# Weight blocks requested one token tile sooner, with a mark before their conversions, and separate staging tiles for the modulation slices

## Chip, cores and metric

The kernel runs on one core of one Trainium2 chip. The metric is the device time of one execution in microseconds (us); the median of several runs is compared.

## The reference

The kernel computes a decoder trunk of two layers on 1024 tokens of width 1024, in float32. Cut to what matters, one layer is

```python
shift, scale, gate = split(c_act @ w_mod + b_mod, 3)
h = rms_norm(x, pre_gain) * (1 + scale) + shift
proj = h @ w_in                      # 1024 x 1024 times 1024 x 3088
# columns of proj: attention (aq, ak, av, ag), retention (rq, rk, rv, rg),
# gated linear attention (gq, gk, gv, gg, ga)
a_out = sliding_window_attention(rot(aq), rot(ak), av, sinks) * silu(ag)
r_out = rms_norm(retention(rot(rq), rot(rk), rv)) * silu(rg)
g_out = rms_norm(gated_linear_attention(gq, gk, gv, log_a(ga)), gain) * silu(gg)
y = concat(a_out, r_out, g_out) @ w_out
x = x + gate * rms_norm(y, post_gain)
```

Attention has 8 heads of 64 with a window of 128 tokens, retention 4 heads of 64 in chunks of 128, gated linear attention 4 heads in chunks. `c_act` is one vector, so that the modulation is a product of one vector with a matrix of 1024 x 3072 for each layer.

## The kernel before

**Units.** The 1024 tokens are eight tiles of 128. The columns of `w_in` and `w_out` are cut into units of 256 columns (`UNITS`): gg, rg, rq, rk, rv, gqk, gv, kv, aq0, aq1, ag0, ag1 and o0 to o3. A unit's weights are held in SBUF as two float32r halves, a high part and a low part (the rest of the rounding), and a product takes three passes: high times high, low times high, high times low (`PASSES`). A tile of a unit is so 3 x 8 matmuls of 128x256 (`project`, line 619), or of 128x512 where the unit is the stationary side (`project_T`).

**Places.** The units lie in a few slots of two large tiles (`arena0`, `arena1`), and each slot serves several units in turn (`PLACE`): gg, rk, gv, aq1 and ag1 one slot, rg, rv, kv, ag0 another, rq, gqk, aq0 a third. A unit can be written only after the last matmul that reads the unit before it in its slot. The order of work in a layer is: gg and rg over all tiles, then for each of four pairs of tiles rq, rk and rv, then gqk, gv and kv, then aq0 and aq1, ag0 and ag1, and the output.

**Loading a unit.** `load` (line 508) makes four requests, one for each chunk of 256 KB. A request has two halves. The first, `issue`, takes a staging tile `st` of 128x512 and issues the chunk's DMA from SyncE's queue. The second, `conv`, writes the high part to the slot (chunk 0 on VectorE, chunks 1 to 3 on ScalarE, lines 149 and 151) and then the low part (chunks 0 to 2 on VectorE, chunk 3 on GpSimd, line 533). With the last chunk it sets the flag `("w", l, name)`, for which `used` (line 504) waits before the unit's first matmul. The requests go through one queue, and the job `loader` (line 474) takes one step each 1.2 us of the planner's clock: an issue, or, when three chunks are in flight (`LAG`, 2, plus 1), first the conversion of the oldest. The call of `load` stands behind the last tile of the unit that held the slot before: in `do_gates` for rk and rv, in the retention loop for gqk, gv and kv, in `do_gqk`, `do_gv` and behind `do_kv` for aq0, aq1 and ag0. These are eight units in each of the two layers. The other units (gg, rg, rq, ag1, o0 to o3, and the last layer's `sw_first`) are requested elsewhere.

**Staging tiles.** There are five `st` tiles (`BST`). They hold the weight chunks, and also the slices of `w_mod`: `mod_third` (line 343) goes through a third of a layer's modulation in two halves of eight slices of 256 KB each; each slice is multiplied by one column of `c_act` and added to `acc` on VectorE (lines 362 and 364). 64 slices come so, at steps of 4.0 us of the planner (`mod2`), from the end of the first layer's gates to the end of the second layer's retention. The post-norm gain (line 377) takes an `st` tile too. Late in the second layer `last_output` uses `st` tiles as scratch and for one operand (`a22`, line 1311).

**What sets the order.** TensorE's instructions run in the order in which the program writes them out. A planner in the kernel makes that order: it has a clock that each matmul advances by an estimate, jobs that wait for a time or a flag, and `pump` (line 210), called every seven matmuls, which runs the jobs that are due. The other engines' instructions and the DMAs are put in order by the framework, in a list made when the program is compiled: it follows the order of the program where several are ready, and waits for tiles to come free. [...] Almost all DMAs are issued by SyncE.

**The retention core**, which the prediction speaks of: `ret_core` (line 1160) transposes a tile of queries and keys on TensorE, copies them out of PSUM on ScalarE (line 1169), multiplies them (the eight matmuls of 64x128), masks the scores on VectorE (line 1179) and adds the state `stR` (lines 1198 and 1200).

## Time and profile before

| what | us |
|---|---|
| median of three runs | 998.21 (996.72 to 999.19) |
| the profiled execution, its own time | 996.31 |
| its span from first to last instruction | 994.6 |
| TensorE busy | 965.7 |
| VectorE busy | 683.2 |
| ScalarE busy | 409.3 |
| GpSimd busy | 246.3 |

The profile is that of the one execution of 996.31 us; 1.7 us of it lie outside the span. PE is TensorE, DVE VectorE, ACT ScalarE, POOL GpSimd, and SPq SyncE's queue of DMA issues. A row of a timeline gives the start, the duration, the engine, the line, the operation, what it writes and reads, the shape, the number of like instructions merged into the row, and in brackets how long the engine was idle before and what ended the wait. A row of a list of waits gives who waited for what, the sum in us, the number of times and the longest. A group of the page's fifth part gives the number of instructions, their busy time in us, the mean of one in ns and the idle time before them. L165 is the helper through which every matmul goes, L180 that of transposes, L149 and L151 those of copies on ScalarE and VectorE, L154 that of DMAs.

### The profile page before, as it was taken

How to read it: one execution, taken by the hardware profiler on the slowest of the kernel's cores; microseconds unless marked ns; L12 is line 12 of the kernel's file. 1: busy time of each engine (PE TensorE's matmuls, PEld its weight loads, DVE VectorE, ACT ScalarE, POOL GpSimd, SP SyncE). 2: the span in 40 equal slices, each digit the busy share in tenths (PEclk: the TensorE clock that was granted, in tenths of full speed). 3: DMA queues.
4: the chain of work that ended last, by engine and by line, in shares of the span. 5: the costliest groups of instructions: out<-in, count | busy, mean ns of one | idle time of the engine just before them, and what ended most of it. 6: DMA issues, size and time to landing. Idle time of an engine off the chain costs nothing.

```text
span 994.6 us, 19641 instructions
## 1 busy us (share of the span) xinstructions
PE 965.7 (97%) x7133; PEld 824.3 (83%) x7133; DVE 683.2 (69%) x1679; ACT 409.3 (41%) x1152; POOL 246.3 (25%) x310
## 2 busy tenths in 40 slices
PE   5899999999999999999999999999999999999996
PEld 1599999888998777778889999988999877777785
DVE  3779857677766777664677286775766577567876
ACT  2477312233332656632555332133333257574222
POOL 2322001233310234420124101113322034545000
PEclk8899999999999999999999999999999999999999
DMA  9843513523135355587555241352122434378883
GB/s 321 290 138 97 159 44 115 177 86 121 61 100 166 91 157 168 170 274 239 189 170 171 69 150 38 118 157 83 53 93 86 127 91 133 112 235 266 267 262 139
DMA packets 112305, 148.77 MB, mean 150 GB/s; under 512 B 12065, under 2 KB 63821, under 8 KB 112209
## 3 DMA queue, kind: packets, MB, share of 16 engines
q1 hardware_dynamic: 106512, 137.96, 44.5%
q10 hardware_dynamic: 5696, 9.56, 2.6%
q8 instruction: 56, 0.92, 0.4%
q14 instruction: 41, 0.33, 0.1%
HBM read 109.20 MB, written 36.18 MB: 146 GB/s over the span
## 4 chain that ended last, share of the span: by engine, by line
PE 80%; DVE 7%; DMA 7%; issue 2%; POOL 1%; ACT 1%; SPq 0%; ACTq 0%; POOLq 0%; DVEq 0%
PE mm L165 61%; PE aux L165 14%; PE aux L180 5%; DMA st<-in_w_in_dram 2%; POOL sm L635 1%; DMA t<-aoS 1%; DMA st<-in_w_last_dram 1%; DMA xk<-in_x_dram 1%; DVE arena L533 1%; DMA a<-mixS 1%; DVE t L1248 0%; DVE t L328 0%; DMA t<-in_x_dram 0%; DMA t<-xs 0%; DMA mixS<-t 0%
## 5 line engine op out<-in xcount | busy, mean ns | idle before, releaser
L165 PE MATMUL mm<-arena 128*128 128x256 f32 (+2 forms) x1824 | 299.9, 318 | 1.8 <-ACT arena L704 1.8
L165 PE MATMUL mm<-arena,arena 128*128 128x256 f32 (+2 forms) x1824 | 298.2, 316 | 0.0
L165 PEld LDWEIGHTS mm<-arena 128*128 128x128 f32 x1824 | 255.5, 191 | 26.0 <-issue 3.3
L165 PEld LDWEIGHTS mm<-arena,arena 128*128 128x128 f32 x1824 | 252.2, 188 | 24.3 <-issue 3.7
L635 POOL TENSOR_TENSOR sm<-sm,mhalf 128x1 f32<-128x1 f32 (+1 forms) x64 | 55.8, 872 | 335.9 <-DVE sm L634 317.8
L165 PE MATMUL mm<-arena,mx 128*128 128x512 f32 (+1 forms) x564 | 130.6, 387 | 0.5 <-ACT kept L1341 0.5
L165 PEld LDWEIGHTS mm<-arena,mx 128*128 128x128 f32 x564 | 101.4, 188 | 24.7 <-issue 1.9
L149 ACT ACTIVATE t<-aux 128x256 f32<-128x256 f32 (+2 forms) x124 | 55.8, 468 | 73.8 <-PE aux L180 62.2
L149 ACT ACTIVATE arena<-st 128x512 fp32r<-128x512 f32 x94 | 56.2, 627 | 53.2 <-DMA st<-in_w_in_dram 19.4
L929 POOL TENSOR_TENSOR smx<-smx,sm 128x512 f32<-128x512 f32 x32 | 36.1, 1129 | 125.7 <-DVE sm L928 118.0
L533 POOL TENSOR_TENSOR arena<-st,arena 128x512 fp32r<-128x512 f32 x31 | 42.7, 1378 | 79.7 <-ACT arena L149 72.9
L533 DVE TENSOR_TENSOR arena<-st,arena 128x512 fp32r<-128x512 f32 x77 | 58.0, 775 | 5.2 <-ACT arena L149 3.3
L925 ACT ACTIVATE smx<-smx,sm 128x129 f32<-128x129 f32 x128 | 49.9, 393 | 25.9 <-DVE sm L922 25.7
L364 DVE SCALAR_TENSOR_TENSOR acc<-st,c_act,acc 128x512 f32<-128x512 f32 x60 | 46.7, 778 | 16.9 <-DMA st<-in_w_mod_dram 16.5
L180 PE MATMUL aux<-c_ident,t 128*128 128x128 f32 (+1 forms) x292 | 48.2, 282 | 5.4 <-DVE t L666 5.0
L180 PEld LDWEIGHTS aux<-c_ident,t 128*128 128x128 f32 (+1 forms) x292 | 35.0, 144 | 12.4 <-DVE t L666 6.9
L698 ACT ACTIVATE t<-aux,mod,mod 128x128 f32<-128x128 f32 x68 | 25.9, 459 | 43.0 <-DVE t L1248 18.1
L165 PEld LDWEIGHTS aux<-t,mx 32*128 32x128 f32 (+1 forms) x896 | 39.5, 187 | 3.9 <-issue 2.1
L973 ACT ACTIVATE t<-aux 128x256 f32<-128x256 f32 x32 | 12.3, 383 | 73.6 <-PE aux L165 65.0
L165 PE MATMUL aux<-t,mx 32*128 32x32 f32 (+1 forms) x896 | 40.7, 272 | 0.0
L920 DVE COPY_PREDICATED smx<-c_curmask,aux 128x256 f32<-128x256 int32 x64 | 25.4, 446 | 19.5 <-ACT smx L149 17.2
L1248 DVE SCALAR_TENSOR_TENSOR t<-t,sm,t 128x512 f32<-128x512 f32 x32 | 24.0, 780 | 18.2 <-DMA t<-in_x_dram 10.8
(224 smaller groups left out, 1387.7 us busy)
## 6 DMA issues: line engine op xcount, KB each, us to landing
st<-in_w_in_dram SPq DMA_DIRECT2D x96, 256.0 KB, 3.8
st<-in_w_mod_dram SPq DMA_DIRECT2D x64, 256.0 KB, 3.1
mx<-mixS SPq DMA_DIRECT2D x20, 512.0 KB, 4.9
mixS<-t SPq DMA_DIRECT2D x72, 128.0 KB, 3.7
st<-in_w_last_dram SPq DMA_DIRECT2D x36, 256.0 KB, 3.8
wm<-in_w_mod_dram SPq DMA_DIRECT2D x12, 512.0 KB, 7.0
t<-in_x_dram SPq DMA_DIRECT2D x24, 256.0 KB, 4.9
t<-tabS SPq DMA_DIRECT2D x16, 256.0 KB, 4.6
```

The lines of the kernel that those rows point to most:

```text
L149: A.activation(dst, src, AF.Copy)
L165: T.matmul(dst, lhsT, rhs, start=start, stop=stop)
L180: T.transpose(dst, src, idn)
L364: V.scalar_tensor_tensor(acc, wt, c_act[:, k:k + 1], acc, ALU.mult, ALU.add)
L533: e.tensor_tensor(lo, st, f(hi), ALU.subtract)
L635: G.tensor_tensor(r, r, mhalf[:, :w], ALU.pow)
L698: A.activation(hf[:, ks], at[kt], AF.Identity, scale=gain, bias=shift)
L920: V.copy_predicated(sv, curmask.unsqueeze(1).to_broadcast((P, 2, P)), pv[:, :, n // P - 1, :])
L925: A.activation(sm[:, h, :], sm[:, h, :], AF.Exp, bias=mx[:, h:h + 1], accum_out=sums[:, h:h + 1])
L929: eng("pn").tensor_tensor(sm[:, :, 0:128], sm[:, :, 0:128], rs.unsqueeze(2).to_broadcast((P, 4, P)), ALU.mult)
L973: A.activation(sq, po, AF.Square)
L1248: V.scalar_tensor_tensor(xt[j], yg[j], r, xt[j], ALU.mult, ALU.add)
```

## The change

1. The eight calls of `load` stand ahead of the last tile's matmuls (for aq0 ahead of the last `project_T`) of the unit that holds the slot, and are followed by a `pump`.
2. Such a request carries a mark, `gate`, the flag `("end", l, name)`. It is set where the call of `load` stood before. The loader issues as long as no more than three chunks are in flight; when it would convert a chunk whose mark isn't set, it waits for the mark.
3. `mod_third` takes its slices and gains from three tiles of their own (`mod_stage`, tag `sm8`, `BMOD`, 3). The five `st` tiles stay.
4. The program is built with `dynamic_dma_scratch_size=1024`.

The planner's delays (`L`), the table of engines (`EN`) and `LAG` stay as they are. The diff, cut where the same edit is repeated:

```diff
+    def mod_stage():
+        return gp.tile([P, 512], F32, tag="sm8", name=nm("ms"), bufs=BMOD)
...
             for k in range(KT):
-                wt = stage()
+                wt = mod_stage()
                 dma("lwm", wt, w_mod[l, j, hh, :, k, :])
...
-                gain = stage()
+                gain = mod_stage()
...
     def convert():
-        conv, st = flying.pop(0)
+        conv, st, gate = flying.pop(0)
+        assert gate is None or gate in flags
         conv(*st)
+
+    def gated():
+        g = flying[0][2]
+        return g is not None and g not in flags
 
     def loader(l):
         while queue or flying:
             if queue:
-                n, issue, conv = queue.pop(0)
-                while flying and sum(len(s) for _, s in flying) + n > LAG + 1:
+                n, issue, conv, gate = queue.pop(0)
+                while flying and sum(len(s) for _, s, _ in flying) + n > LAG + 1:
+                    if gated():
+                        yield (0.0, flying[0][2])
                     convert()
-                flying.append((conv, issue()))
+                flying.append((conv, issue(), gate))
                 yield lat("ld1", l)
             else:
+                if gated():
+                    yield (0.0, flying[0][2])
                 convert()
                 yield lat("ld2", l)
...
         def do_gates(name, p):
             w = used(l, name)
             for t in (2 * p, 2 * p + 1):
+                if t == NT - 1:
+                    load(l, "rk" if name == "gg" else "rv", gate=("end", l, name))
+                    pump()
                 pg = mm()
...
             if p == NP_ - 1:
-                load(l, "rk" if name == "gg" else "rv")
+                flag(("end", l, name))
...
                 for tt in range(2):
                     t = 2 * p + tt
+                    if t == NT - 1:
+                        load(l, {"rq": "gqk", "rk": "gv", "rv": "kv"}[name], gate=("end", l, name))
+                        pump()
                     pm = mm()
...
-                if last:
-                    load(l, {"rq": "gqk", "rk": "gv", "rv": "kv"}[name])
+                if t == NT - 1:
+                    flag(("end", l, name))
...
-B2, B1, BS, BST, MMB, SMB = 10, 8, 11, 5, 3, 3
+B2, B1, BS, BST, MMB, SMB, BMOD = 10, 8, 11, 5, 3, 3, 3
...
-    nc = _bacc.Bacc("TRN2", target_bir_lowering=False, num_devices=1)
+    nc = _bacc.Bacc("TRN2", target_bir_lowering=False, num_devices=1, dynamic_dma_scratch_size=1024)
```

`do_gqk`, `do_gv` and `do_kv` are changed like `do_gates`, with aq0, aq1 and ag0.

More of the change, by code (lines that the diff above doesn't have):

```diff
@@ L490, in drain, with request @@
         while queue:
-            n, issue, conv = queue.pop(0)
-            while flying and sum(len(s) for _, s in flying) + n > LAG + 1:
+            n, issue, conv, gate = queue.pop(0)
+            while flying and sum(len(s) for _, s, _ in flying) + n > LAG + 1:
                 convert()
-            flying.append((conv, issue()))
+            flying.append((conv, issue(), gate))
         while flying:
             convert()
-    def request(l, n, issue, conv):
-        queue.append((n, issue, conv))
+    def request(l, n, issue, conv, gate=None):
+        queue.append((n, issue, conv, gate))
         if not loading[0]:
@@ L506, in used, with load @@
         return unit(l, name)
-    def load(l, name, first=None):
+    def load(l, name, first=None, gate=None):
         if l >= DEPTH:
@@ L547, in load @@
             else:
-                request(l, 1, lambda kc=kc: issue(kc), lambda st, kc=kc: conv(kc, st))
+                request(l, 1, lambda kc=kc: issue(kc), lambda st, kc=kc: conv(kc, st), gate)
     def sw(name):
@@ L1502, in layer @@
         for p in range(NP_):
-            last = p == NP_ - 1
             rr = {}
@@ L1526, in do_gqk @@
         def do_gqk(hf, kk):
+            if hf and kk:
+                load(l, "aq0", gate=("end", l, "gqk"))
+                pump()
             pm = mm()
@@ L1538, in do_gqk @@
             if hf and kk:
-                load(l, "aq0")
+                flag(("end", l, "gqk"))
         def do_gv(p):
             for t in (2 * p, 2 * p + 1):
+                if t == NT - 1:
+                    load(l, "aq1", gate=("end", l, "gv"))
+                    pump()
                 pm = mm()
@@ L1550, in do_gv @@
             if p == NP_ - 1:
-                load(l, "aq1")
+                flag(("end", l, "gv"))
         def do_kv(p):
@@ L1556, in do_kv @@
             for t in (2 * p, 2 * p + 1):
+                if t == NT - 1:
+                    load(l, "ag0", gate=("end", l, "kv"))
+                    pump()
                 pk = mm()
@@ L1572, in layer @@
             do_kv(p)
-        load(l, "ag0")
+        flag(("end", l, "kv"))
         job(attn_run(l))
```

## The prediction

> **What bounds the kernel now.** I read the page's first part, then TensorE's waits after the start-up, then the timelines of the engines around the longest of them.
>
> ```profile
> span 994.6 us, 19641 instructions
> PE 965.7 (97%) x7133; PEld 824.3 (83%) x7133; DVE 683.2 (69%) x1679; ACT 409.3 (41%) x1152; POOL 246.3 (25%) x310
> 50.00:994.60 944.60, 930.03 (x6994) 805.15 (x6992) 654.60 (x1615) 390.66 (x1107) 231.02 (x287) 1.00 0.46 141
> ```
> ```profile
> PE aux L165 <- ACT t L149: 3.0, 3, 1.3
> PE mm L165 <- DMA a<-mixS: 1.5, 1, 1.5
> PE mm L165 <- ACT kept L1341: 0.5, 1, 0.5
> PE aux L165 <- DVE sm L634: 0.4, 1, 0.4
> PE aux L165 <- DVE t L1179: 0.4, 1, 0.4
> PE aux L165 <- DVE stR L1200: 0.3, 1, 0.3
> PE aux L180 <- DVE mx L1121: 0.2, 1, 0.2
> ```
>
> TensorE is the bound. Past 50 us it is busy for 930.03 of 944.60 us at a granted clock of 1.00, and the second fence, which is every wait of TensorE over 0.15 us in that stretch, adds up to 3.0 + 1.5 + 0.5 + 0.4 + 0.4 + 0.3 + 0.2 = 6.3 us. The change removes no matmul, so it can give back only a part of these 6.3 us. The page's chain of waits also names DMA of in_w_in_dram with 2% of the span (some 20 us), but most of that time lies beside a running TensorE, so I take the waits and not the chain as the measure.
>
> Which of them have to do with weights? These are TensorE's rows with an idle time, first layer and second layer, and ScalarE (ACT) just ahead of them.
>
> ```profile
> 192.83 0.71 PE L165 MATMUL aux<-t 64*128 64x128 f32 x8 [1.29 <-ACT t L149]
> ...
> 663.09 0.71 PE L165 MATMUL aux<-t 64*128 64x128 f32 x8 [0.54 <-ACT t L149]
> ...
> 669.66 0.71 PE L165 MATMUL aux<-t 64*128 64x128 f32 x8 [1.22 <-ACT t L149]
> ...
> 673.62 0.46 PE L165 MATMUL aux<-stR,t 128*128 128x128 f32 x2 [0.30 <-DVE stR L1200]
> ...
> 674.62 0.43 PE L165 MATMUL aux<-t,t 128*128 128x64 f32 x2 [0.37 <-DVE t L1179]
> ```
> ```profile
> 189.35 0.63 ACT L149 ACTIVATE arena<-st 128x512 fp32r<-128x512 f32 x1 [1.72 <-DMA st<-in_w_in_dram]
> ...
> 191.39 0.63 ACT L149 ACTIVATE arena<-st 128x512 fp32r<-128x512 f32 x1 [1.14 <-DMA st<-in_w_in_dram]
> ```
> ```profile
> 661.10 0.63 ACT L149 ACTIVATE arena<-st 128x512 fp32r<-128x512 f32 x1 [0.90 <-DMA st<-in_w_in_dram]
> 661.64 0.64 ACT L149 ACTIVATE t<-aux 128x256 f32<-128x256 f32 x2
> ...
> 668.49 0.63 ACT L149 ACTIVATE arena<-st 128x512 fp32r<-128x512 f32 x1 [3.71 <-DMA st<-in_w_in_dram]
> 669.03 0.58 ACT L149 ACTIVATE t<-aux 128x512 f32<-128x512 f32 x1
> ```
>
> The reader is to see a queue. The eight 64x128 matmuls are the retention scores (ret_core), and they need the copy of line 1169. That copy stands on ScalarE behind the conversion of a weight chunk, and the conversion stands still until the chunk's DMA has landed: 3.71 us at 668.49, 1.72 and 1.14 us at 189.35 and 191.39. No matmul needs those weights yet; they only sit ahead of something that a matmul does need. The two VectorE waits at 673.62 and 674.62 follow in the same place, where VectorE too was held by late chunks. So the part of the 6.3 us that this change aims at is 1.29 + 0.54 + 1.22 + 0.30 + 0.37 = **3.72 us**, all of it in the last retention pair of the two layers.
>
> **Why those chunks are late.** SyncE's timeline shows when they are asked for.
>
> ```profile
> 155.72 0.33 SPq L154 DMA_DIRECT2D st<-in_w_in_dram  x1
> ...
> 161.96 0.33 SPq L154 DMA_DIRECT2D st<-in_w_mod_dram  x1
> 162.75 4.50 SPq L154 DMA_DIRECT2D st<-in_w_in_dram  x3
> ...
> 171.64 0.33 SPq L154 DMA_DIRECT2D st<-in_w_mod_dram  x1
> ...
> 174.34 0.33 SPq L154 DMA_DIRECT2D st<-in_w_mod_dram  x1
> ...
> 181.84 4.82 SPq L154 DMA_DIRECT2D st<-in_w_in_dram  x3
> ...
> 187.24 0.38 SPq L154 DMA_DIRECT2D st<-in_w_in_dram  x1
> ```
> ```profile
> SPq L154 <- DVE arena L533: 7.3, 6, 3.4
> SPq L154 <- DVE acc L364: 6.9, 5, 3.9
> ```
> ```profile
> 170.20 1.68 ACT L149 ACTIVATE arena<-st 128x512 fp32r<-128x512 f32 x3 [3.70 <-PE mm L165]
> ```
>
> gqk's chunks are issued from 155.72 on, though the call that asks for them stands behind rq's last tile, whose matmuls end at 170.2 (the conversions wait for them there). The issue is thus already some 14 us ahead of its place in the code: what holds it is a free staging tile, not the request. Between 160 and 200 us SyncE stands 7.3 us until a conversion's low half (L533) and 6.9 us until a modulation product (L364) gives a tile back. kv's four chunks go out at 181.84 to 187.24 and are wanted at 187 to 190.
>
> **The change part by part.**
>
> *Three staging tiles for the modulation slices.* Nothing is computed that wasn't; 64 slices and 4 gains move to their own tiles, the five old ones hold weights alone. At 181.84 the queue was let go by a modulation product, so the last chunks go out earlier by about the time of the tiles lent out: three slices sit between gqk's and kv's chunks, up to the 6.9 us above. The waits of 1.1 to 3.7 us on landing are shorter than that, so I count them as gone, with TensorE's 3.72 us behind them. Three tiles instead of a share of five could starve the slices.
>
> ```profile
> L364 DVE SCALAR_TENSOR_TENSOR acc<-st,c_act,acc 128x512 f32<-128x512 f32 x60 | 46.7, 778 | 16.9 <-DMA st<-in_w_mod_dram 16.5
> ...
> st<-in_w_in_dram SPq DMA_DIRECT2D x96, 256.0 KB, 3.8
> st<-in_w_mod_dram SPq DMA_DIRECT2D x64, 256.0 KB, 3.1
> ```
>
> A slice lands 3.1 us after its issue and its product takes 0.78 us, so three tiles carry a slice every (3.1 + 0.8) / 3 = 1.3 us; the planner spaces them by 4.0 us (mod2). VectorE already waits 16.5 us for slices, and TensorE's seven waits name none of these products. Cost: nothing, hidden by VectorE's own idle third; between -0.4 us (the one wait on L634 goes too) and +1.3 us (a slice on the path of one retention tile).
>
> *Requests one tile sooner.* Sixteen requests (rk, rv, gqk, gv, kv, aq0, aq1, ag0 in two layers) stand ahead of the last project instead of behind it. At most three chunks are issued before the mark (LAG), the fourth after it. By 155.72 against 170.2 above the issues are not held by the request, so by itself this is worth nothing. SyncE's queue keeps its number of DMAs; the four issues of a request, 0.33 us each, can only move ahead of stores of mixS and loads of srS, and no wait of TensorE in the list above names those. The pump that comes with a request runs at the clock of the pump before it, so only the loader moves in it, and the loader emits no matmul and no clock: TensorE's order stays as it is.
>
> *The mark.* Before, a unit's four conversions came 3.6 to 7.2 us behind the request in the planner's clock (steps of 1.2, ld1 and ld2); now the first comes at the first pump after the mark, the last about 3 us sooner than before. In the lists of ScalarE, VectorE and GpSimd they so come ahead of work that stood ahead of them. Each still waits for the last tile's matmuls. Behind the waiting conversion stand ScalarE's copies out of PSUM, and for these TensorE waits. A unit's conversions are three on ScalarE at 0.63 us, one cast and three low halves on VectorE and one low half on GpSimd:
>
> ```profile
> L533 DVE TENSOR_TENSOR arena<-st,arena 128x512 fp32r<-128x512 f32 x77 | 58.0, 775 | 5.2 <-ACT arena L149 3.3
> ```
>
> On VectorE three times 0.78 us come sooner, ahead of rotations that the scores want later; there the planner leaves room, since a key's rotation is done two tiles before its scores. No row shows a mark. Its price is between nothing and one wait like that at 669.66 (1.22 us) for each of 16 units, 19.5 us. I take three ends that cost what 663.09 cost, 3 x 0.54 = 1.6 us, since the conversions at 170.20 stood 3.70 us behind TensorE and cost TensorE nothing: nearer the low end.
>
> *Descriptor scratch cut to 1024.*
>
> ```profile
> q1 hardware_dynamic: 106512, 137.96, 44.5%
> q10 hardware_dynamic: 5696, 9.56, 2.6%
> ```
>
> The program's DMAs run on these two hardware queues, issued by SyncE and ScalarE, and its table of issuing engines (EN) gives none to GpSimd, so I count nothing. [...]
>
> **Sum.** -3.72 + 1.6 = -2.1 us: span 992.5, the execution's own time 996.31 - 2.1 = 994.2. That execution was 1.9 us under the median of the three runs (998.21, they lie from 996.72 to 999.19); from the median, **996.1 us**. A difference under 0.3%, 3.0 us, I take as no change that can be told.
>
> **Rivals.**
>
> *All of it comes (0.30).* The mark costs nothing, as at 170.20: 998.21 - 3.7 = 994.5, or 993.0 if one more of the other waits goes (a<-mixS, 1.5). For it: these conversions run at the same release before and after.
>
> *The low halves hold the ring, not the slices (0.17).* The 7.3 us behind L533 are the larger of the two rows, and 187.24 was let go by such a half. Then kv's last chunk still lands near 191 and the 1.29 and 0.54 stay; 1.9 goes, 1.6 comes: 997.9. That the sooner request does not bring the data sooner belongs here.
>
> *ScalarE stands behind TensorE in place of the DMA (0.15, slower).* A marked conversion at the head of ScalarE's queue, as at 170.20, with a copy for the scores or an attention tile behind it: 1.2 us an end. From the third end on it eats the gain, from six on it is a loss over 0.3%: 6 x 1.25 - 3.7 = +3.8, 1002.0. Against it: TensorE's waits show no such case in 16 ends.
>
> *VectorE and GpSimd in each other's way (0.05).*
>
> ```profile
> 178.23 0.42 DVE L979 TENSOR_TENSOR t<-t,t 128x256 f32<-128x256 f32 x1
> ...
> 183.39 0.85 DVE L979 TENSOR_TENSOR t<-t,t 128x256 f32<-128x256 f32 x1
> ```
> ```profile
> 182.65 1.30 POOL L533 TENSOR_TENSOR arena<-st,arena 128x512 fp32r<-128x512 f32 x1
> ```
>
> The same instruction takes 0.42 us alone and 0.85 us beside GpSimd's low half. If the sooner conversions bring every unit's GpSimd half beside an instruction that TensorE waits for, that is 16 x 0.43 = 6.9, less 3.7: 1001.4. The number of such halves does not change and most of them delay nothing that TensorE wants, hence the small chance. [...]
>
> **Numbers.** My forecast has 0.33, the rivals 0.30, 0.17, 0.15 and 0.05 with it make one. Under 995.2 lies most of the first rival and a little of the forecast: faster 0.33. Over 1001.2 lies most of the third and half of the fourth: slower 0.17. Within 0.3%: 0.50. The range goes from the low end of the first rival, 993.0, to 1001.0, which leaves out most of the two slow cases and little else.
>
> **What would show it.** Right: kv's last chunk is issued before 184 us in the first layer and before 661 in the second; ScalarE's waits for in_w_in_dram in those pairs are gone; TensorE's waits at 193, 663 and 670 as well, and its list after 50 us is near 4 us. Wrong: new rows of TensorE waiting on ACT L149 with ScalarE waiting on PE mm ahead of them (third rival), chunks let go by L533 as late as now (second), or VectorE's products waiting longer than 16.5 us with TensorE behind them. Outside all this would be a span that falls by more than the 6.3 us of waits.

## The result and the profile after

The changed kernel takes 1009.45 us (median of six runs, 1006.92 to 1014.10), the kernel before beside it 997.81 (996.56 to 999.19): a ratio of 1.0121, with a 95% interval of 1.0102 to 1.0141, so **12 us slower**. The forecast was 996.1, and its range ended at 1001.0.

The first two lines are the page of the changed kernel, the third is its row of the windows view for the time past 50 us (busy time of PE, PEld, DVE, ACT, POOL, then the granted clock, the transfers' share and GB/s); the second fence is its list of TensorE's waits in that time.

```profile
span 1005.2 us, 19645 instructions
PE 969.1 (96%) x7133; PEld 826.9 (82%) x7133; DVE 681.5 (68%) x1679; ACT 409.7 (41%) x1152; POOL 246.4 (25%) x310
50.00:1005.20 955.20, 934.82 (x6999) 808.94 (x6997) 653.59 (x1617) 391.60 (x1109) 231.60 (x288) 0.99 0.46 140
```
```profile
PE aux L183 <- DVE t L678: 5.3, 2, 4.0
PE aux L168 <- ACT t L152: 2.1, 2, 1.2
PE mm L168 <- DMA a<-mixS: 1.6, 2, 1.4
PE aux L168 <- DVE t L1191: 1.5, 1, 1.5
PE aux L168 <- DVE mx L1133: 0.4, 1, 0.4
```

The five engines do the same number of instructions (the counts in the second line are those of before); past 50 us the stretch is 955.20 - 944.60 = 10.6 us longer. TensorE idles 955.20 - 934.82 = 20.4 us there in place of 14.6, so **5.8 us are new waits**; and it is busy for 4.8 us longer with the same matmuls, at a mean clock of 0.99 in place of 1.00, so **4.8 us are slower matmuls**. That second half has no place in the prediction at all. It isn't peculiar to the profiled run: the mean granted clock is 0.985 over the changed kernel's six runs and 0.990 over the 91 runs of the kernel before that were taken beside the experiments. Counting what is missing to 1.00 as time at half clock, that is 30 us against 19, so about 6 of the 12 us (my estimate).

**The waits.** The row of 5.3 us is new: two waits (1.22 and 4.04 us) at the hand-over of the layers, where the second layer's rows are normalised (L678; L666 before) as the first layer's output comes out. The row for L152 and the one for L1191 are the second layer's last retention pair. TensorE and ScalarE there, in the changed kernel:

```profile
672.96 0.71 PE L168 MATMUL aux<-t 64*128 64x128 f32 x8 [0.89 <-ACT t L152]
678.20 0.77 PE L168 MATMUL aux<-t,t 128*128 128x64 f32 x4 [1.46 <-DVE t L1191]
681.38 0.71 PE L168 MATMUL aux<-t 64*128 64x128 f32 x8 [1.24 <-ACT t L152]
```
```profile
670.97 0.63 ACT L152 ACTIVATE arena<-st 128x512 fp32r<-128x512 f32 x1 [3.34 <-DMA st<-in_w_in_dram]
676.46 0.63 ACT L152 ACTIVATE arena<-st 128x512 fp32r<-128x512 f32 x1 [3.56 <-DMA st<-in_w_in_dram]
```

The picture is that of before, and larger: 0.89 + 1.46 + 1.24 = 3.59 us where 2.43 stood, and ScalarE still stands on chunks that haven't landed. Only the first layer's 1.29 us at 193 is gone.

**The hand-over.** SyncE's rows, of the kernel before and then of the changed one:

```profile
447.65 0.33 SPq L154 DMA_DIRECT2D aoS<-t  x1
450.22 0.93 SPq L154 DMA_DIRECT2D t<-aoS  x2
...
451.79 0.86 SPq L154 DMA_DIRECT2D t<-in_x_dram  x2
...
486.69 0.98 SPq L154 DMA_DIRECT2D t<-in_x_dram  x2
```
```profile
443.62 1.09 SPq L157 DMA_DIRECT2D ms<-in_w_mod_dram  x2
...
449.59 0.33 SPq L157 DMA_DIRECT2D aoS<-t  x1
454.65 0.93 SPq L157 DMA_DIRECT2D t<-aoS  x2
...
456.22 0.86 SPq L157 DMA_DIRECT2D t<-in_x_dram  x2
...
489.84 1.12 SPq L157 DMA_DIRECT2D ms<-in_w_mod_dram  x2
491.05 1.67 SPq L157 DMA_DIRECT2D t<-in_x_dram  x2
...
493.72 1.27 SPq L157 DMA_DIRECT2D ms<-in_w_mod_dram  x2
```

SyncE's longest wait from 484 to 492 us in the changed kernel, and the two waits behind it:

```profile
SPq L157 <- DVE sm L652: 5.3, 1, 5.3
```
```profile
498.96 0.75 DVE L1260 SCALAR_TENSOR_TENSOR t<-t,sm,t 128x512 f32<-128x512 f32 x1 [3.36 <-DMA t<-in_x_dram]
```
```profile
508.96 1.97 PE L183 MATMUL aux<-c_ident,t 128*128 128x128 f32 x8 [4.04 <-DVE t L678]
```

In the kernel before no slice is loaded between 435.8 and 534.4 us: the last part's slices share the five tiles with weight chunks and stand behind them. With tiles of their own they are free to go, and the list that the framework writes for SyncE puts them among the loads of the residual `x`. The store of an attention tile goes out 1.9 us later, its reload and the load of `x` behind it 4.4 us later (456.22 against 451.79), while TensorE is 1.1 us late there (its transposes at 456.1 against 455.0). Then SyncE stands 5.3 us, up to 489.84, before the next two slices. The list names a small VectorE instruction; the slice's product that gives a tile back ends at the same moment (VectorE's row at 489.07 lasts 0.74 us), so I read it as a wait for one of the slices' own three tiles. The load of `x` stands behind, and goes out at 491.05 where it was 486.69. Two more slices follow it at 493.72, so four slices of 256 KB are issued within 5 us, around it. Its second half, issued at 492.39, lands 6.6 us later (498.96) and VectorE stands 3.36 us for it; in the kernel before VectorE had both halves at 490.96, 4.3 us after the first was issued, without a wait for them. The fifth token tile is late by that, and TensorE waits 4.04 us. VectorE also has five products of slices to do from 489.07 to 507.3, about 3.7 us that it did not have there before; no run separates them from the loads.

**The clock.** Three stretches of the windows view behind that wait:

```profile
504.60:508.00 3.40, 0.32 (x2) 0.00 (x0) 3.37 (x9) 3.14 (x10) 0.48 (x1) 1.00 0.75 253
508.00:511.40 3.40, 2.44 (x10) 2.34 (x11) 2.98 (x8) 1.63 (x6) 0.39 (x1) 0.51 0.53 192
511.40:514.80 3.40, 3.40 (x9) 2.62 (x9) 2.95 (x6) 0.91 (x2) 0.99 (x1) 0.50 0.45 162
```

From 508.0 on, for 6.8 us, the granted clock is 0.50, and in the last of the three stretches nine matmuls fill what sixteen filled before. In the kernel before no such stretch lies between 46 and 991 us (granted clock 1.00).

### The profile page after: what moved, and what is told of

Same layout as the page of the kernel before. It is cut to its first block, busy times and chain, and to the rows that moved or that the text cites. A ratio compares the mean times of both kernels' runs of the same rounds, so it can differ in the third digit from the quotient of the medians.

```text
span 1005.2 us, 19645 instructions
## 1 busy us (share of the span) xinstructions
PE 969.1 (96%) x7133; PEld 826.9 (82%) x7133; DVE 681.5 (68%) x1679; ACT 409.7 (41%) x1152; POOL 246.4 (25%) x310
## 4 chain that ended last, share of the span: by engine, by line
PE 62%; DMA 8%; DVE 8%; ACT 2%; issue 2%; POOL 1%; SPq 0%; ACTq 0%; POOLq 0%; DVEq 0%
PE mm L168 46%; PE aux L168 13%; PE aux L183 3%; DMA t<-in_x_dram 2%; DMA st<-in_w_in_dram 1%; DMA st<-in_w_last_dram 1%; DMA t<-aoS 1%; POOL sm L647 1%; DVE t L1260 1%; DMA ms<-in_w_mod_dram 1%; DMA aoS<-t 1%; DMA a<-mixS 1%; DMA t<-mixF 1%; ACT t L710 1%; DVE acc L367 1%
## 5 line engine op out<-in xcount | busy, mean ns | idle before, releaser
L152 ACT ACTIVATE t<-aux 128x256 f32<-128x256 f32 (+2 forms) x124 | 55.9, 468 | 77.1 <-PE aux L183 61.2
L152 ACT ACTIVATE arena<-st 128x512 fp32r<-128x512 f32 x94 | 56.1, 628 | 56.4 <-PE mm L168 22.6
L545 DVE TENSOR_TENSOR arena<-st,arena 128x512 fp32r<-128x512 f32 x77 | 58.7, 786 | 6.1 <-ACT arena L152 4.3
L545 POOL TENSOR_TENSOR arena<-st,arena 128x512 fp32r<-128x512 f32 x31 | 43.5, 1403 | 78.6 <-ACT arena L152 69.8
L367 DVE SCALAR_TENSOR_TENSOR acc<-ms,c_act,acc 128x512 f32<-128x512 f32 x60 | 46.0, 767 | 15.9 <-DMA ms<-in_w_mod_dram 15.4
```

The costliest lines, as they stand in the source:

```text
L152: A.activation(dst, src, AF.Copy)
L367: V.scalar_tensor_tensor(acc, wt, c_act[:, k:k + 1], acc, ALU.mult, ALU.add)
L545: e.tensor_tensor(lo, st, f(hi), ALU.subtract)
```

## The experiments

Three theories. **A**: the slices' own tiles cost, since they take a brake off the slices, whose loads and products now run ahead into the hand-over and into the first core of the gated attention. **B**: the mark costs, since the conversions stand earlier in ScalarE's, VectorE's and GpSimd's lists than their chunks land. **C**, in the first two expectations: half from each. In those of e8_delay, e10_fill_after and e11_fill_start C is the name of another theory, formed after the first four profiles: a wait costs more than itself because the clock is halved after it. All runs of the kernel before with other tiles also have the smaller scratch; e13_scratch_only tells what that alone does. Ratios are to runs of the kernel before on the same chip (997.8, 997.4, 996.6, 996.7, 997.1 and 997.2 us in the six groups of runs), with their 95% interval.

### One part alone, and parts of the first part

**e1_tiles_only.** The kernel before with the own tiles (and the smaller scratch), no mark.

```diff
-                wt = stage()
+                wt = mod_stage()
...
-                gain = stage()
+                gain = mod_stage()
```

> The kernel before with the modulation slices in three tiles of their own and the smaller descriptor scratch, requests and marks as before. Theory A (the own tiles let the last layer's modulation slices run ahead into the change from the first layer to the second, where they stand before the loads of x on SyncE's queue and before the residual on VectorE): slower by most of the 11.6 us, 1006 to 1011, with a wait of TensorE of 3 us or more on DVE t (the normalised rows) near 505 us, a stretch at half the granted clock behind it, and slices issued before 500 us. Theory B (the marked conversions or the shifted requests delay ScalarE and VectorE): within 0.3% of before, 995 to 1001. Theory C (both parts cost a half each): 1002 to 1005.

1009.96 us, 1.0142 (1.0109 to 1.0175): **the whole loss**, with TensorE's order unchanged. TensorE waits 2.43 us at the hand-over, 0.89 us at 222 us, and 0.95 + 1.42 + 1.32 us in the second layer's last retention pair. The half clock that theory A expected behind the hand-over isn't there: the 56 matmuls of 128x512 behind that wait take 13.29 us from 510.84 on, 13.27 in the kernel before. In this profile it stands at 224.8 us (0.50 up to 228.2), and behind the last pair's last wait, from 680.97 on, twelve matmuls of 128x512 take 5.14 us where the kernel before has 3.02.

**e2_mark_only.** The changed kernel with slices and gains back in the shared tiles.

```diff
-                wt = mod_stage()
+                wt = stage()
...
-                gain = mod_stage()
+                gain = stage()
```

> The changed kernel with the modulation slices back in the five shared tiles; requests one tile sooner and marks stay. Theory A: no loss of the kind, 994 to 1000, and no half clock between 50 and 900 us. Theory B: 1006 to 1011. Theory C: 1002 to 1005. Either way the chunks of kv should not be issued earlier than before by more than 2 us, since a free tile holds them and not the request.

1008.05 us, 1.0112 (1.0087 to 1.0137). No wait at the hand-over; but 3.62 us at 197, and in the second layer's last pair 0.38, 1.35 and 2.16:

```profile
676.02 0.63 ACT L152 ACTIVATE arena<-st 128x512 fp32r<-128x512 f32 x1 [3.83 <-DMA st<-in_w_in_dram]
...
679.79 0.63 ACT L152 ACTIVATE arena<-st 128x512 fp32r<-128x512 f32 x1 [1.85 <-DMA st<-in_w_in_dram]
```
```profile
683.73 0.43 PE L168 MATMUL aux<-t,t 128*128 128x64 f32 x2 [2.16 <-DVE t L1191]
```

Each part alone costs about what both cost together (by the medians 10 and 12 against 12 us), so the two do not add up; half from each is out. Theory A had 994 to 1000 us here, so it is not the whole account.

**e3_last_gate_shared.** The changed kernel with the last layer's third part (the gate's 16 slices and 2 gains) back in the shared tiles. **e4_held.** The changed kernel with that part's loads placed behind the first layer's last load of `x`.

```diff
-                wt = mod_stage()
+                wt = mod_stage() if (l, j) != (1, 2) else stage()
```
```diff
+                if (l, j) == (1, 2):
+                    with tc.issue_after(lastx[0].ins):
+                        dma("lwm", wt, w_mod[l, j, hh, :, k, :])
```

> The changed kernel, but the sixteen gate slices of the second layer take the five shared tiles again, where they must stand in turn behind the weight chunks asked for before them. The other 48 slices keep their own tiles. Theory A: the wait of TensorE near 505 us and the half clock behind it vanish, 996 to 1002. Theory B: unchanged, 1006 to 1011.

> The changed kernel with all own tiles, but each DMA of the second layer's gate slices is placed on SyncE's queue behind the first layer's last load of x. Theory A: as in the kernel with the shared tiles for these slices or better, 995 to 1001, with the slices issued after 515 us and no half clock near 505. If the slices' products alone and not their place before the loads of x were the cause this gives the same, since the products follow the slices. Theory B: 1006 to 1011.

1003.66 us, 1.0065 (1.0042 to 1.0087), and 1005.22, 1.0084 (1.0063 to 1.0105). In both the hand-over is clean; in the profile of e4_held the transposes come at 503.98 without a wait:

```profile
503.98 1.03 PE L183 MATMUL aux<-c_ident,t 128*128 128x128 f32 x8
```

Theory A had up to 1002 and up to 1001 us, so it foretold more than came; theory B had 1006 to 1011, too much, if by little for e4_held. 4 to 6 of the 12 us hang on where that part's loads stand. The hold moves the slices' products along with their loads, so it doesn't tell the two apart; that VectorE stands 3.36 us for `x` speaks for the loads.

**e9_first_own.** As e1_tiles_only, with the last layer's third part on the shared tiles (the edit of e3_last_gate_shared, no mark). **e14_tiles_held.** As e1_tiles_only, with the hold of e4_held. **e13_scratch_only.** The kernel before with the smaller scratch alone.

> The kernel before with the three own tiles and no mark, but the last layer's third modulation part (the gate and its gains) left on the shared tiles. Theory A with its place at the hand-over: against the 1010 of the own tiles alone, the waits at 472 and 510 go (0.33 and 2.43 us) and what is left is the wait of 0.89 at 222 with its half clock, so 999 to 1004 us. If the whole loss of the own tiles came from the last layer's third part: 995 to 998 us. If it came from the first layer's slices: 1006 to 1010 us.

> The three own tiles, no mark, and the loads of the last layer's third modulation part placed behind the last load of the first layer's residual tiles on SyncE's list. Theory A, as refined by the profiles (SyncE stood 5.3 us at 484 to 490 us on a slice's load that waited for its own tile, with the residual's loads queued behind it): against the 1010 of the own tiles alone, the waits at 473 and 510 go and it is 1001 to 1005 us, near the 1000.5 of the run in which those slices stayed on the shared tiles. If the slices' products on VectorE, not their loads on SyncE, made the rows late: still 1007 to 1010.

> The kernel before with only the smaller GpSimd scratch of the change (1024), which stands in every run with own or more tiles and in those with the mark; no instruction differs. The prediction's step (the scratch costs nothing): 996 to 998.5 us. If the scratch itself costs, the readings of those runs fall by as much.

1000.46 us, 1.0037 (1.0016 to 1.0058); 1005.44, 1.0084 (1.0054 to 1.0114); 997.90, 1.0010 (0.9993 to 1.0028). The scratch costs nothing that can be told. Without the mark the last third part on own tiles costs 9 us by the medians (10 by the ratios, 1.0142 - 1.0037); moving its loads out of the hand-over gives back 3 to 6 (1.0142 - 1.0084 is the larger; one of the four runs of e1_tiles_only, 1016.14 us, draws its ratio up). In the profile the hold brings a new wait of 1.25 us at 540, and the last pair's 0.96 + 1.35 + 1.13 us are about what they were; why the rest of the loss stays is not shown. With the loads held, the mark adds nothing (e4_held and e14_tiles_held have the same ratio).

### The mark

**e6_mark_late.** As e2_mark_only, with the conversions let go 3.6 us of the planner's clock after the marked end, about where they stood before.

```diff
-        return g is not None and g not in flags
+        return g is not None and (g not in flags or flags[g] > clk[0])
...
-                flag(("end", l, name))
+                flag(("end", l, name), 3.6)
```

> The mark alone (slices in the shared five tiles), but the conversions are let go 3.6 us of the list's reckoning after the marked end, about where they stood before. Theory B (with the mark the conversions stand earlier in ScalarE's, VectorE's and GpSimd's lists than their chunks land, and each list stands behind them): the time falls from the 1008 of the mark alone to 996 to 1000 us, and the waits of 1.35 and 2.16 us in the last retention pair of the second layer and of 3.62 at 197 go back to the 0.4 to 1.3 of the kernel before. Rival (the earlier requests themselves, or the changed order of TensorE, cost): it stays at 1004 to 1009 us.

1005.17 us, 1.0082 (1.0066 to 1.0098): 3 of the 11 us come back, with intervals that overlap a little. In the profile the last pair's waits are shorter (0.60, 1.02, 0.88 and 0.37), and the 3.62 us at 197 is 2.27 at 195. The time lies in the rival's range: B is at most a part of the mark's cost, and the larger part is not where the conversions stand.

**e15_held_late.** The changed kernel with both cures, the hold of e4_held and the lateness of e6_mark_late.

> The changed kernel with both cures: the last part's loads held behind the residual's, and the conversions let go 3.6 us later. If the two losses are separate and each cure gives what it gave alone (4 and 3 us): 1001 to 1004 us. If the conversions' place costs only where the slices sit on the shared tiles (the chunks then come late, which the own tiles mend): 1004 to 1006, as with the loads held alone.

1006.54 us, 1.0089 (1.0059 to 1.0119), against 1.0084 with the hold alone. The late conversions give nothing here that can be told: on own tiles their place is not what costs.

### How many tiles, and for whom

**e5_eight_shared**, **e16_six_shared**: the kernel before with eight or six shared tiles (`BST`). **e12_one_own**: own tiles without the mark, with one tile for the slices and seven for the weights.

> The kernel before with eight shared staging tiles in place of five; no mark, no tile of the slices' own. Theory A (what lets the modulation slices run ahead costs: their products and loads come in a burst and push the normalised rows of the hand-over back): slices may now run up to three tiles further ahead, so waits of 1 to 4 us at 222 and at 505 to 512 as in the run with the own tiles alone, and 1002 to 1010 us. The step of the prediction that named the ring as what holds kv's chunks: they are asked for earlier, the 1.29 us at 193 and the 1.22 and 0.54 of the last pair of the second layer fall under 0.4, and if A is wrong the time is 993 to 996 us. [...]

> The kernel before with six shared tiles, no mark and no own tile. With eight it was 1002.9, with the ring's waits in the second layer's last retention pair gone (some 3 us) and 222 and 538 us worse by 8. If the loss grows with how far the slices may run ahead: half of each or less, so 996 to 1000 us, and the first wait at 193 and the pair's are smaller than before's. If any change of the order of the loads around the slices costs (the list's reckoning was fitted to five): 1001 to 1005 us.

> The kernel before with one tile of the slices' own and seven for the weight chunks, and no mark. With one tile a slice's load must wait for the product before it, about as in the kernel before; the weight chunks have all seven and wait for no slice. If the run-ahead of the slices is what the own tiles cost, and the ring's hold on kv's chunks is what they can save (as the eight shared tiles saved the last pair's 3 us): no wait above 0.5 us at 222, at 510 and in the last retention pairs, and 993 to 997 us. Rival (VectorE now stands at the head of its list for each slice's load, some 2 us each, 56 slices): waits for VectorE's results all along and 1000 us or more.

1002.93 us, 1.0054 (1.0037 to 1.0072); 1000.76, 1.0047 (1.0029 to 1.0064); 1009.79, 1.0121 (1.0095 to 1.0147). With eight tiles ScalarE converts the second layer's chunks with no wait for a transfer, and TensorE's timeline shows no wait between 655 and 690 us:

```profile
663.40 1.68 ACT L149 ACTIVATE arena<-st 128x512 fp32r<-128x512 f32 x3 [1.05 <-PE mm L165]
669.73 1.68 ACT L149 ACTIVATE arena<-st 128x512 fp32r<-128x512 f32 x3
```

So the ring of tiles was what held the second layer's chunks; in the first layer's last pair 0.88 us of the 1.29 stay. But the slices use the same room: at the first core of the gated attention seven of their products run on VectorE within 9 us (212.5 to 221.4) where they took 23 (211.9 to 235.1), TensorE waits 1.22 us at 221.75 and 2.3 at 538, and the loss is larger than the gain. Six tiles come out between their two expectations, with 0.81 us at 221, 1.72 at 537 and still 1.12 in the last pair. One own tile goes wrong the other way. SyncE's waits from 470 to 548 us:

```profile
SPq L157 <- DVE sm L637: 15.3, 5, 5.6
SPq L157 <- DMA ms<-in_w_mod_dram: 15.3, 5, 5.7
```
```profile
546.78 1.59 PE L183 MATMUL aux<-c_ident,t 128*128 128x128 f32 x8 [2.72 <-DVE t L669]
```

SyncE stands on slices' loads that wait for their one tile (L637's small instruction comes right behind a slice's product, as at the hand-over above), with the loads of `x` and `mixS` behind them. Slower slices don't help as long as they stand there in SyncE's list.

**e17_kv_own**, **e18_kv_own_last**, **e19_kv_four**. The kernel before, slices and all, with tiles of their own for kv's chunks alone: three in both layers, three in the second layer only, four in both layers. The edit shown is that of e19_kv_four.

```diff
+    def kv_stage():
+        return gp.tile([P, 512], F32, tag="sk", name=nm("sk"), bufs=4)
...
-            st = stage().rearrange("p (k n) -> p k n", k=2)
+            st = (kv_stage() if name == "kv" else stage()).rearrange("p (k n) -> p k n", k=2)
```

> The kernel before with three staging tiles of their own for kv's chunks alone (both layers); slices, gains and all other chunks share the five as before, and there is no mark. What the last pair of each layer waits for is kv's chunks, and nothing is given to the slices but the four places that kv's chunks leave. If the run-ahead of the slices is the price and the ring's hold the prize: the waits of 1.29 at 193, 0.54, 1.22, 0.30 and 0.37 at 663 to 675 fall under 0.3 each and it is 993 to 996 us, under the kernel before. If any shift of the loads around it costs as six and eight shared tiles did: 998 to 1002 us, with waits at 222 or 537.

> As the run before it, but for kv's chunks of the second layer alone; everything up to 630 us stays as it was. If the chunks' tiles are what the second layer's last pair waits for: its 0.54, 1.22, 0.30 and 0.37 go, 2.4 us, and it is 994 to 996 us. If those chunks would still land late (their turn on SyncE's list or among the transfers): 996 to 998 us with the waits unchanged.

997.00 us, 1.0003 (0.9989 to 1.0017), and 998.03, 1.0009 (0.9994 to 1.0023): no difference that can be told; neither expectation had the waits right. They moved. ScalarE and TensorE of e17_kv_own:

```profile
670.50 0.63 ACT L152 ACTIVATE arena<-sk 128x512 fp32r<-128x512 f32 x1 [4.96 <-DMA sk<-in_w_in_dram]
671.04 0.36 ACT L976 ACTIVATE t<-aux 128x256 f32<-128x256 f32 x1
```
```profile
673.48 0.46 PE L168 MATMUL aux<-stR,t 128*128 128x128 f32 x2 [2.24 <-DVE stR L1203]
```

The scores come 2.1 us earlier, but kv's fourth chunk waits for the tile of the first, and behind its conversion stands the square of the retention's output (L976), VectorE's work on that and on `stR`, and then TensorE: 2.24 us, what had been won.

> As the run with kv's chunks in three tiles of their own, but with four, one for each chunk. With three, the last pair's 1.22 and 0.30 went and a wait of 2.24 us came at 673: ScalarE stood 4.96 us on the fourth chunk, which had to wait for the first one's tile, and the retention's square stood behind it. If the tile is all that made this chunk late: no wait over 0.5 us in either layer's last pair, and 993 to 996 us, under the kernel before (997). If the chunk's turn on SyncE's list makes it late anyway: 996.5 to 998 us, with the wait still there.

**993.77 us, 0.9968 (0.9953 to 0.9983): faster than both kernels, by 3.4 us.** TensorE's order is that of the kernel before. Its waits past 50 us, the loads of kv's chunks, ScalarE's conversions of them, and the window past 50 us:

```profile
PE mm L168 <- DMA a<-mixS: 1.4, 1, 1.4
PE mm L168 <- ACT kept L1344: 1.3, 1, 1.3
PE aux L168 <- DVE sm L637: 0.8, 1, 0.8
PE aux L168 <- DVE t L1182: 0.5, 1, 0.5
PE aux L183 <- DVE mx L1124: 0.2, 1, 0.2
```
```profile
67.28 1.11 SPq L157 DMA_DIRECT2D sk<-in_w_in_dram  x2
...
190.02 1.40 SPq L157 DMA_DIRECT2D sk<-in_w_in_dram  x3
```
```profile
185.79 1.67 ACT L152 ACTIVATE arena<-sk 128x512 fp32r<-128x512 f32 x3
...
661.64 1.69 ACT L152 ACTIVATE arena<-sk 128x512 fp32r<-128x512 f32 x3
```
```profile
50.00:992.20 942.20, 929.67 (x6992) 805.05 (x6990) 657.26 (x1614) 390.77 (x1107) 231.53 (x287) 1.00 0.46 142
```

ScalarE's row is gone from the list: the chunks have landed when their conversions come up. Of the 3.72 us only 0.5 (L1182) is left. The loads did not just come a little sooner. With their tiles free, the framework's list puts them far ahead: the first layer's four go out at 67 to 72 us, for conversions at 186, and the second layer's at 190 to 194, as soon as the first layer's conversions give the tiles back, for conversions at 662. With three tiles the second layer's fourth chunk went out at 664.62, since no tile was left for it. So this run gives kv's loads a place far from the crowded one; that one tile a chunk would do as much for loads that stay near their use, no run shows.

### The clock

**e8_delay.** The kernel before, with the two scalings of the fifth token tile's rows at the hand-over done six times over.

```diff
-                V.tensor_scalar(xn[j], xt[j], r, None, ALU.mult)
+                for _ in range(NREP if (l, t) == (1, 4) else 1):
+                    V.tensor_scalar(xn[j], xt[j], r, None, ALU.mult)
```

> The kernel before with one thing added: the two scalings of the fifth token tile's rows at the hand-over (0.48 us each, at 499 and 500 us) are done six times over, with the same result, so VectorE gets 4.85 us more work there and TensorE should wait some 3 to 3.5 us at 502, near the 4.04 us that the changed kernel waits there. Theory C (such a wait costs more than itself, since the clock granted to TensorE halves for 3.4 or 6.8 us after it): a half-clock stretch behind the wait, and 1001 to 1005 us, the wait and 1.6 to 3.3 us beside it. Rival (a wait costs itself at most, and later slack may take it back): 998 to 1001.5 us and no half-clock stretch.

1002.52 us, 1.0049 (1.0031 to 1.0067): 5 us, with two new waits of 2.24 us together in the profile.

```profile
504.78 0.66 PE L180 MATMUL aux<-c_ident,t 128*128 128x128 f32 x4 [1.51 <-DVE t L667]
506.17 1.12 PE L180 MATMUL aux<-c_ident,t 128*128 128x128 f32 x4 [0.73 <-DVE t L667]
```
```profile
502.70:506.10 3.40, 1.23 (x7) 0.55 (x5) 3.40 (x10) 0.57 (x2) 0.00 (x0) 1.00 0.85 296
506.10:509.50 3.40, 3.33 (x10) 2.85 (x11) 2.45 (x8) 1.56 (x4) 0.55 (x1) 0.50 0.18 72
```

With the same order of matmuls, the profile of this run is 0.9 us behind the kernel before ahead of the waits (the 19 matmuls there start at 498.66 us, 497.79 before) and 5.1 us when the first 30 matmuls of 128x512 behind them are done (515.33, 510.25 before): the two waits cost 4.2 us there, 2.0 us more than their length. The whole run is 5.1 us longer by the medians (1002.52 against 997.41), so what the stretch at half clock took wasn't made up here.

**e10_fill_after.** The changed kernel with 24 useless transposes of the identity ahead of the fifth tile's transposes. **e11_fill_start.** The kernel before with such transposes in four waits of its first 41 us.

```diff
+    def fill(dst, n):
+        for _ in range(n):
+            T.transpose(dst[:, 0:P], ident, ident)
...
                 x = aux()
+                if (l, t, j) == (1, 4, 0):
+                    fill(x, 24)
```

> The changed kernel with 24 useless transposes of the identity (128x128, about 0.11 us each, 2.7 us) put on TensorE ahead of the fifth token tile's transposes at the hand-over of the layers, where it waits 4.04 us; they write the bank that those transposes then overwrite. The wait's end, set by VectorE's rows, doesn't move. Theory C (the clock granted is halved for the next stretch when the matmuls of a 3.4 us stretch before were too few): no half-clock stretch at 508, and 1.6 to 3.4 us less than the changed kernel's 1009.5, so 1005.5 to 1008. Rival (the lateness of the rows alone costs, or the half clock comes from elsewhere): 1009 to 1010 us with the half-clock stretch still there.

> The kernel before with such useless transposes in the four waits of its first 41 us: 24 and 8 ahead of the first and second token tile's transposes (waits of 3.19 and 1.28 us), 8 ahead of the last column sums of the first modulation (1.17), 14 ahead of the first projection (1.80). Nothing of the change is in it. Theory C: the half-clock stretches at 18.3 and 38.8 (6.8 us each) go or shorten; the 8 modulation matmuls that took 4.85 us take about 3.5 and the 27 projection matmuls that took 6.01 about 3.3, so up to 4 us less, 993 to 996 us. Rival (the start is bound by loads, VectorE and ScalarE, whatever TensorE's clock): 997 to 998.5 us, the same time with longer waits in place of the half clock. If the useless work stands in the way: 999 us or more.

In e10_fill_after the half clock at 508 is gone; two others stand in its profile:

```profile
508.40:511.80 3.40, 3.07 (x23) 2.61 (x21) 2.96 (x7) 0.66 (x3) 0.65 (x1) 1.00 0.63 231
```
```profile
219.70:223.10 3.40, 3.15 (x62) 2.83 (x61) 3.40 (x9) 1.35 (x7) 0.62 (x1) 0.99 0.53 174
223.10:226.50 3.40, 3.40 (x18) 3.40 (x18) 2.86 (x8) 0.10 (x1) 1.89 (x5) 0.50 0.32 104
```

It takes 1009.91 us, 1.0131 (1.0115 to 1.0147), no less than the changed kernel. So with TensorE kept at work through the wait the clock behind it stays up, 1.00 where the changed kernel has 0.51 and 0.50, in this one profile (the last section sets it beside others); that the changed kernel as a whole gets faster without the stretch is not shown: my 1.6 to 3.4 us didn't come, and in this run other places, at 223 and 677, were halved instead. e11_fill_start takes 998.10 us, 1.0014 (0.9998 to 1.0030), a miss as well: the granted clock is 1.00 from 18.3 to 25.1 us and from 38.8 to 45.6, where the kernel before has 0.50, the mean clock rises from 0.991 to 0.996, and TensorE only waits longer (busy for 2.37 of the 4.40 us from 45.6 to 50, 3.88 before). At the start TensorE isn't the bound, so its clock is worth nothing there that can be told.

## Why the prediction was wrong

- **"Three staging tiles ... Cost: nothing, hidden by VectorE's own idle third"** is the step that failed: the range given for it ended at +1.3 us, and that part alone costs 12.2 us (e1_tiles_only, 1009.96 against 997.77). I asked whether three tiles could starve the slices and whether VectorE had room for them. The danger was the other one: what a slice's load does to the loads behind it on SyncE's list. Waiting behind weight chunks was what kept 16 slices out of the hand-over and spread the products at the gated attention. Without the mark, 9 of the 12 us hang on the tiles of those 16 slices (e9_first_own), 3 to 6 of these on their loads' place at the hand-over (e14_tiles_held); the rest is spread over waits in several places and is **not settled**. I weighed what the four issues of a request can move ahead of, and not what the slices' loads can, though SyncE's list with its gap in slice loads from 435.8 to 534.4 us was there to be read.
- **"-3.72 us"**: the size was right and the means wrong. "What holds it is a free staging tile, not the request" holds (eight tiles, and e19_kv_four with its 3.4 us). That it is the slices that hold them does not: with the slices gone, SyncE still stands for low halves (L545), 8.5 us for GpSimd's and 4.8 for VectorE's between 160 and 200 us, where L533's row had 7.3; that is the second rival. In the changed kernel the first layer's 1.29 us went, and the second layer's 2.43 became 3.59.
- **"Requests one tile sooner ... worth nothing"** was right in that kv's chunks were issued no earlier: from 185.2 us on in place of 181.8, and from 673.0 in place of 663.0 (where TensorE was 9.9 us late). What the sooner requests cost by themselves isn't known, since every run with the mark has both.
- **"TensorE's order stays as it is"** was wrong. With the mark, transposes and score matmuls move by seven matmuls in a few places, mostly from 108 to 161 us. What that costs was not measured by itself.
- **The mark's 1.6 us** was mis-sized where it stands alone, 10 to 11 us, of which about 3 come back with late conversions. The other 7 to 8 are **not settled**: beside the own tiles the mark costs between nothing (changed kernel against e1_tiles_only; e4_held against e14_tiles_held) and 3 us (e3_last_gate_shared against e9_first_own, intervals that overlap). My slow rival, ScalarE standing behind TensorE, isn't what the waits show: ScalarE stands on transfers.
- **The clock** was taken as a constant 1.00. That left out what new waits can cost beside their own length: 4.8 of the 10.6 us.
- **The scratch** costs nothing, as predicted: with it alone 997.90 us, a ratio of 1.0010 (e13_scratch_only). Why it should matter which engine issues the DMAs, as "so I count nothing" takes for granted, no run shows.

## What to carry to other kernels

A tile that one stream must wait for may be the only thing that keeps it out of another stream's way: before giving a stream its own buffers, look in the DMA queue for the stretch where it is now absent, and name what would stand behind it. Give the buffers to the transfer that is late, one for each of its chunks (kv's four tiles: 3.4 us), not to the one that is in its way; then look where the list has put the loads, which may be hundreds of us ahead. And reckon with a wait of TensorE in the middle of a kernel costing more than its length: in e8_delay 2.24 us of waits cost 4.2, with the granted clock at 0.50 for 3.4 us behind them.

## What the runs showed of the hardware

In the profile of the kernel before the granted clock is 0.50 from 18.3 to 25.1 us, from 38.8 to 45.6 and from 991.1 to the end; in that of the changed kernel from 16.5 to 26.8, from 40.4 to 43.8, from 508.0 to 514.9 and from 999.6 to the end. The stretches before the end last 6.8, 6.8, 10.2, 3.4 and 6.8 us, and between them the granted clock is 1.00. In e8_delay it is 0.50 from 506.1 to 509.5, 3.4 us.

What TensorE did in the 3.4 us ahead of such a stretch, and in some that none follows:

| run, us | TensorE busy, us | matmuls | granted clock in the stretch behind |
|---|---|---|---|
| after, 504.6 to 508.0 | 0.32 | 2 | 0.51 |
| before, 14.9 to 18.3 | 0.49 | 4 | 0.50 |
| e10_fill_after, 673.6 to 677.0 | 1.19 | 7 | 0.51 |
| e8_delay, 502.7 to 506.1 | 1.23 | 7 | 0.50 |
| e1_tiles_only, 221.4 to 224.8 | 2.51 | 58 | 0.50 |
| before, 35.4 to 38.8 | 2.73 | 20 | 0.50 |
| e10_fill_after, 219.7 to 223.1 | 3.15 | 62 | 0.50 |
| e10_fill_after, 508.4 to 511.8 | 3.07 | 23 | 1.00 |
| e11_fill_start, 14.9 to 18.3 | 3.32 | 26 | 1.00 |
| before, 218.0 to 221.4 | 3.40 | 64 | 1.00 |
| e10_fill_after, 505.0 to 508.4 | 3.40 | 26 | 1.00 |

The four with the least work, 0.32 to 1.23 us, all have the half clock behind them. Busy time alone doesn't part the rest: 3.15 us with 62 matmuls has it behind and 3.07 us with 23 has not. Nor does the number of matmuls: 58 and 62 have it, 64 have not. In e1_tiles_only at least 54 of the 58 are matmuls of 32x32. The 24 useless transposes of e10_fill_after, 2.78 us from 506.51 on, fall on its stretches from 505.0 and from 508.4.

In the kernel before TensorE does little but matmuls with one column of weights from 29.3 to 34.6 us (twelve in 5.31 us), and the granted clock is 1.00 until 38.8. And a wait doesn't always bring the half clock: the 2.43 us at the hand-over in e1_tiles_only have the 13.29 us for 56 matmuls behind them, the 2.24 us in e8_delay the 0.50. What decides was not shown. The clock goes some way to explain how e3_last_gate_shared could take from 997 to 1007 us: its two fastest runs have a mean clock of 0.990, its slowest 0.984, which is 12 us more at half clock, so some 6 of the 10 us (my estimate).
